# Two sums of each block of the second feed-forward weight, made in DRAM by GpSimd's DMAs

## Chip, cores and metric

The kernel runs on one core of a Trainium2 chip. The core has a matrix engine (TensorE, PE in the rows), VectorE (DVE), ScalarE (ACT), GpSimd (POOL), SyncE (SP) and 16 DMA engines that all queues share. The metric is the device time of one execution in microseconds (us). Every engine works through its own list of instructions in order; an instruction that waits holds all that stand behind it on that engine. A DMA that adds to its destination is issued from POOL.

## What is computed

One decoder layer on 512 tokens of width 2048, in float32:

```python
proj = jnp.einsum("bsd,de->bse", x, w_in[l])
q, k, v, gate_b, gate_c, h = jnp.split(proj, split_pts, axis=-1)
q, k = rope(q), rope(k)
attn = sliding_window_gqa(q, k, v, attn_sinks[l])
conv = gate_b * causal_depthwise_conv(gate_c * h, short_conv_w[l])
y = jnp.einsum("bsm,md->bsd", jnp.concatenate([attn, conv], -1), w_out[l])
x = layer_norm(DEEPNORM_ALPHA * x + y, ln1_g[l], ln1_b[l])
u = causal_depthwise_conv(jnp.einsum("bsd,df->bsf", x, ffn_w_up[l]), ffn_conv_w[l])
a, g = jnp.split(u, 2, axis=-1)
y = jnp.einsum("bsf,fd->bsd", jax.nn.silu(a) * g, ffn_w_down[l])
x = layer_norm(DEEPNORM_ALPHA * x + y, ln2_g[l], ln2_b[l])
```

## The kernel before

Every float32 operand is split into a high and a low part (`split`, L181 to L184: ScalarE casts `whi`, then VectorE subtracts to get `wlo`), and a product is three matmuls. Weights come as chunks of 1 MB, 128 x 2048, in the DRAM tensor `ws`. SP loads them into three `raw` buffers (`dma_to`); four pairs of `whi`/`wlo` hold 1024 columns each, so PE has at most four halves of a chunk prepared.

The stages are these. First the projection to q, in two panels of eight halves, with the one for k and v (four halves) between them. Each of the three ends with the rotation (`rope`, L249 to L261): per token block VectorE writes `wa` and `wb` from PSUM and POOL adds them into `qm` (for q) or `kr` (for k). `wa` and `wb` have two buffers each, so VectorE cannot begin the third token block before POOL has added the first. Then follow the convolution's projections, 48 halves, with attention woven in: attention's first step (`att_q`) splits `qm`, and PE transposes the parts `qs` right behind the first of the 48 halves. Then come the output projection, LayerNorm, the up-projection, and the down-projection with the second LayerNorm.

Up- and down-projection use seven products in place of eight on a 2 x 2 block of sub-matrices (Strassen's scheme in Winograd's form). In the down-projection a block `n` (10 of them, `NB`) has four weight chunks, w0 to w3, and products 1 to 7. Products 1, 2 and 3 use w0, w1 and w2. Product 5 uses w3 + w0, product 6 adds w2 to that, product 4 adds w1 to that, and product 7 uses w3 + w2. The products run in the order 1, 2, 6, 3, 7, 5 of the next block, 4.

Before the change the sums are made in SBUF. `d_load` has POOL load w3 into a buffer `wqd` and add w0 by two DMAs (`d_add`, half a chunk each). For product 6 VectorE adds w2 from its `raw` buffer (L566), once for each half. For product 4 POOL adds w1 by DMA. For product 7 SP loads w3 into a `raw` buffer and POOL adds w2 by two DMAs there.

The order of instructions on each engine is fixed when the program is built, by a scheduler that estimates when each could run; a DMA call stands in the program where that scheduler sets it, not where the Python line is.

Of the kernel before, what the change touches and what calls it, by code (L numbers as in the profile page):

```python
# [8 lines left out]
F32 = mybir.dt.float32  # L9
F32R = mybir.dt.float32r  # L10
AF = mybir.ActivationFunctionType
ALU = mybir.AluOpType
AX = mybir.AxisListType

P = 128
S = 512
D = 2048
# [21 lines left out]
C_DOWN = C_UP + 2 * NF  # L39
ND = NF // 4  # L40
NB = 2 * (NF // 8)
C_TAIL = C_DOWN + 4 * NB
# [75 lines left out]
class Kernel:  # L118
# [19 lines left out]
    def dma_to(self, c):  # L138
        nc = self.nc
        while self.next_dma <= min(c, NCHUNK - 1):  # L140
            i = self.next_dma
            t = self.p_raw.tile([P, 2048], F32, name="raw")
            self.raw[i] = t
            self.next_dma += 1

            cuts = {0: (512, 1024, 1536, 2048), 1: (1024, 2048)}.get(i, (2048,))
            c0 = 0
            for c1 in cuts:
                nc.sync.dma_start(t[:, c0:c1], self.ws_d[i][:, c0:c1])
                if i == 0:  # L150
                    k = c0 // 512 % 2
                    self.load_x(slice(k, k + 1), nc.scalar if c0 < 1024 else nc.sync)
                else:
                    self.load_x()
                c0 = c1
            if C_UP <= i < C_DOWN and (i - C_UP) % 2:
                self.w_add(t[:, 1024:], (i - C_UP) // 2, 1, 0)
            if C_DOWN <= i < C_TAIL and (i - C_DOWN) % 4 == 3:
                for h in range(2):
                    self.d_add(t, (i - C_DOWN) // 4, 2, h)  # L160

    def load_x(self, ks=slice(0, 2), queue=None):
        if self.x_at < KT // 2:
# [378 lines left out]
    def d_add(self, t, n, i, h):  # L542

        c = slice(1024 * h, 1024 * (h + 1))
        self.nc.gpsimd.dma_start(t[:, c], self.ws_d[C_DOWN + 4 * n + i][:, c], accum_op=ALU.add)

    def d_load(self, n):

        if n < NB:
            t = self.wq[n] = self.p_qd.tile([P, 2048], F32, name="wqd")  # L550
            self.nc.gpsimd.dma_start(t, self.ws_d[C_DOWN + 4 * n + 3])
            for h in range(2):
                self.d_add(t, n, 0, h)

    def down_prep(self, n, p, h):

        if p in (5, 6, 4):
            src = self.wq[n]
        else:
            c = C_DOWN + 4 * n + (1, 2, 3, 7).index(p)  # L560
            self.dma_to(c + 2)
            src = self.raw[c]
        hi, lo = self.hl_tiles()
        cs = slice(1024 * h, 1024 * (h + 1))
        if p == 6:
            self.nc.vector.tensor_tensor(src[:, cs], src[:, cs], self.raw[C_DOWN + 4 * n + 2][:, cs], op=ALU.add)  # L566
        self.split(hi, lo, src[:, cs])
        self.hl[n, p, h] = (hi, lo)
        if p == 6:
            self.d_add(src, n, 1, h)  # L570
        elif h and p == 4:
            del self.wq[n]
            self.d_load(n + 2)
        elif h and p in (1, 2, 3, 7):
            del self.raw[c]
# [147 lines left out]
    def run(self):  # L723
        nc, tc = self.nc, self.tc
# [17 lines left out]
        p_d = opened("spill", 1, space=bass.MemoryType.DRAM)  # L742
        self.hd = [p_d.tile([P, 4, S], F32, name=f"hd{u}") for u in range(ND)]
        zd = [p_d.tile([P, D], F32, name=f"zd{tb}") for tb in range(NTB)]
        self.x_at, self.xraw = 0, {}
        self.dma_to(2)

# [59 lines left out]
        for i in range(2 * NC_CONV):  # L807
            j = 2 * C_CONV + i
            q = i % 4
            if q == 0:  # L810
                pss = [self.psum("mm") for _ in range(2)]
            hi, lo = self.half(j, 4)
            self.feat_half(hi, lo, q, pss)
            if q == 3:
                self.conv_evac(i // 4, pss)
            for u, off in ((i, 0), (i - 1, 1), (i - 4, 2), (i - 5, 3)):
                if u % 2 == 0 and 0 <= u // 2 < 16:
                    n = u // 2
                    if off == 0:
                        st[n] = self.att_q(*units[n])  # L820
                    elif off == 1:
                        st[n] = self.att_scores(*units[n], st[n])
                    elif off == 2:
                        st[n] = self.att_transpose(*units[n], st[n])
                    else:
                        self.att_values(*units[n], st.pop(n))
# [10 lines left out]
        for k in (slice(0, 2), slice(2, 8)):  # L837
            for tb in range(NTB):
                sl = slice(tb * P, (tb + 1) * P)
                src = self.qm[tb].rearrange("p (k t) -> p k t", t=P)  # L840
# [75 lines left out]
        n = len(self.order)  # L916
# [28 lines left out]
        for i, (m, p, h) in enumerate(self.todo[n:]):  # L945
            self.prepare(n + i + 4)
            u, c = divmod(m, 2)
# [8 lines left out]
            if u + 1 < NB // 2:  # L956
                at, q = (1, {3: 4, 7: 5, 4: 1, 11: 2, 12: 6, 16: 3, 13: 7})
                if u == 0:
                    at, q = (3, {4: 4, 11: 5, 12: 1, 16: 2, 13: 6, 17: 3, 14: 7})
# [17 lines left out]
            k = end.index((m, p))  # L977
# [41 lines left out]
```

## Time and profile before

| | |
|---|---|
| median of 3 runs | 2019.3 us (2015.41 to 2021.93) |
| the profiled execution | 2018.78 us |
| its span, first to last instruction | 2016.7 us |
| mean granted TensorE clock | 0.980 |
| PE busy | 1928.5 us (96%) |
| DVE, ACT, POOL busy | 1405.6, 918.8, 286.3 us |
| DMA moved | 398.73 MB, 198 GB/s over the span |

A row of a timeline gives start, length, engine, line and operation, and in brackets the idle time before it and what ended that. A row of the windows gives for a stretch how long each engine was busy, the granted clock, the mean busy share of the 16 DMA engines and the rate they moved. The table of queues gives packets, megabytes and the share of the 16 engines' time: q0 holds the DMAs that POOL issues, q1 those of SP and ACT.

### The profile page before, as it was taken

How to read it: one execution, taken by the hardware profiler on the slowest of the kernel's cores; microseconds unless marked ns; L12 is line 12 of the kernel's file. 1: busy time of each engine (PE TensorE's matmuls, PEld its weight loads, DVE VectorE, ACT ScalarE, POOL GpSimd, SP SyncE). 2: the span in 40 equal slices, each digit the busy share in tenths (PEclk: the TensorE clock that was granted, in tenths of full speed). 3: DMA queues.
4: the chain of work that ended last, by engine and by line, in shares of the span. 5: the costliest groups of instructions: out<-in, count | busy, mean ns of one | idle time of the engine just before them, and what ended most of it. 6: DMA issues, size and time to landing. Idle time of an engine off the chain costs nothing. (4 is left out here: it accounts for less than half of the span.)

```text
span 2016.7 us, 25991 instructions
## 1 busy us (share of the span) xinstructions
PE 1928.5 (96%) x9950; PEld 1638.4 (81%) x9950; DVE 1405.6 (70%) x2001; ACT 918.8 (46%) x1403; POOL 286.3 (14%) x315
## 2 busy tenths in 40 slices
PE   9999999999994899999999999999997989999887
PEld 7988888888893788888888888888885778787766
DVE  5357676353358777777777777777777778787777
ACT  4234444232124555555555555555555544344331
POOL 1110000000033111111111111111111111111104
PEclk9999999999996999999999999999998999999989
DMA  6222122552234599999999999999998868888762
GB/s 264 101 88 84 63 84 75 156 219 94 105 110 130 145 263 253 266 240 263 250 258 259 243 261 248 262 246 258 255 238 238 247 194 242 220 233 245 237 188 84
DMA packets 93499, 398.73 MB, mean 198 GB/s; under 512 B 9472, under 2 KB 20768, under 8 KB 67520
## 3 DMA queue, kind: packets, MB, share of 16 engines
q0 software_dynamic: 36256, 139.11, 36.2%
q1 hardware_dynamic: 56544, 256.92, 34.2%
q8 instruction: 78, 1.28, 0.2%
q10 hardware_dynamic: 576, 1.05, 0.1%
q14 instruction: 45, 0.37, 0.0%
HBM read 377.12 MB, written 19.92 MB: 197 GB/s over the span
## 5 line engine op out<-in xcount | busy, mean ns | idle before, releaser
L184 DVE TENSOR_TENSOR wlo<-raw,whi 128x1024 fp32r<-128x1024 f32 (+1 forms) x358 | 438.2, 1227 | 293.2 <-ACT whi L183 292.8
L183 ACT CAST whi<-raw 128x1024 fp32r<-128x1024 f32 (+1 forms) x358 | 373.5, 1045 | 574.9 <-PE mm L216 118.3
L482 PE MATMUL mm<-act,whi 128*128 128x512 f32 x1072 | 385.0, 400 | 0.0
L484 PE MATMUL mm<-act,wlo 128*128 128x256 f32 x1072 | 302.1, 282 | 0.0
L482 PE MATMUL aux<-x,whi 128*128 128x512 f32 x704 | 252.7, 395 | 20.9 <-DVE x L184 20.0
L482 PEld LDWEIGHTS mm<-act,whi 128*128 128x128 f32 x1072 | 202.7, 189 | 49.7 <-DVE mt L490 0.2
L434 POOL DMA_DIRECT2D wq<-ws x132 | 129.5, 983 | 726.0 <-DVE wlo L184 605.7
L184 DVE TENSOR_TENSOR wlo<-wq,whi 128x1024 fp32r<-128x1024 f32 x132 | 161.1, 1223 | 98.6 <-ACT whi L183 98.4
L484 PEld LDWEIGHTS mm<-act,wlo 128*128 128x128 f32 x1072 | 204.0, 190 | 0.4 <-DVE wlo L184 0.3
L183 ACT CAST whi<-wq 128x1024 fp32r<-128x1024 f32 x132 | 138.2, 1050 | 139.4 <-PE mm L482 50.3
L484 PE MATMUL aux<-x,wlo 128*128 128x256 f32 x704 | 199.6, 284 | 0.0
L482 PEld LDWEIGHTS aux<-x,whi 128*128 128x128 f32 x704 | 133.1, 189 | 52.1 <-DVE x L184 20.3
L214 PE MATMUL mm<-act,whi 128*128 128x512 f32 x384 | 151.5, 394 | 0.0
L216 PE MATMUL mm<-act,wlo 128*128 128x512 f32 x384 | 150.1, 391 | 0.0
L215 PE MATMUL mm<-act,whi 128*128 128x512 f32 x384 | 149.6, 390 | 0.0
L484 PEld LDWEIGHTS aux<-x,wlo 128*128 128x128 f32 x704 | 133.2, 189 | 0.2
L482 PE MATMUL mm<-x,whi 128*128 128x512 f32 x352 | 125.5, 393 | 2.3 <-DVE m L490 1.2
L614 PE MATMUL mm<-whi,act 128*128 128x512 f32 x256 | 103.5, 405 | 21.4 <-DVE z L630 21.4
L482 PE MATMUL aux<-act,whi 128*128 128x512 f32 x336 | 120.4, 398 | 0.0
L214 PE MATMUL mm<-whi,act 128*128 128x512 f32 (+1 forms) x316 | 116.5, 369 | 0.0
L216 PE MATMUL mm<-whi,act 128*128 128x512 f32 (+1 forms) x316 | 116.2, 368 | 0.0
L215 PE MATMUL mm<-wlo,act 128*128 128x512 f32 (+1 forms) x316 | 116.2, 368 | 0.0
(202 smaller groups left out, 3837.0 us busy)
## 6 DMA issues: line engine op xcount, KB each, us to landing
raw<-ws SPq DMA_DIRECT2D x180, 1024.0 KB, 8.2
wq<-ws POOLq DMA_DIRECT2D x132, 512.0 KB, 9.3
raw<-ws POOLq DMA_DIRECT2D x64, 512.0 KB, 7.6
wq<-ws SPq DMA_DIRECT2D x44, 512.0 KB, 8.2
wqd<-ws POOLq DMA_DIRECT2D x40, 512.0 KB, 13.2
hd<-ca SPq DMA_DIRECT2D x44, 256.0 KB, 10.0
h<-hd SPq DMA_DIRECT2D x22, 512.0 KB, 12.8
wqd<-ws POOLq DMA_DIRECT2D x10, 1024.0 KB, 5.1
```

The lines of the kernel that those rows point to most:

```text
L183: self.nc.scalar.copy(hi, src)
L184: self.nc.vector.tensor_tensor(lo, src, hi.bitcast(F32), op=ALU.subtract)
L214: mm(ps, sh, mh, start=start, stop=False)
L215: mm(ps, sh, ml, start=False, stop=False)
L216: mm(ps, sl, mh, start=False, stop=stop)
L434: self.nc.gpsimd.dma_start(dst, self.ws_d[C_UP + 2 * f + i][:, 1024 * j:1024 * (j + 1)], accum_op=ALU.add)
L482: mm(ps, hi[:, sl], x[:, k, :, :].rearrange("p a t -> p (a t)"), start=new and k == 0, stop=False, skip_group_check=not new)
L484: mm(ps[:, :H], lo[:, sl], x[:, k, 0, :], start=False, stop=k == 7, skip_group_check=not new)
L614: mm(ps[b], xh, hi[:, k, :], start=new and h == 0 and k == 0, stop=False, **kw)
```

## The change

Twenty tensors `sum0_5`, `sum0_7`, ..., `sum9_7` of 1 MB each are set up in DRAM. `w_sum` copies w3 of a block from `ws` to such a tensor (one DMA) and adds w0 or w2 to it (two DMAs of half a chunk), all issued from POOL, DRAM to DRAM: 20 copies and 40 adds. It is called in the loop over the convolution's 48 halves. `d_load` then loads w3 + w0 in one DMA, and SP loads w3 + w2 in place of w3. VectorE's add of w2 for product 6 becomes two DMA adds on POOL, issued when product 5's halves are split.

```diff
             for c1 in cuts:
-                nc.sync.dma_start(t[:, c0:c1], self.ws_d[i][:, c0:c1])
+                n, q = divmod(i - C_DOWN, 4)
+                src = self.sums[n, 7] if C_DOWN <= i < C_TAIL and q == 3 else self.ws_d[i]
+                nc.sync.dma_start(t[:, c0:c1], src[:, c0:c1])
...
-            if C_DOWN <= i < C_TAIL and (i - C_DOWN) % 4 == 3:
-                for h in range(2):
-                    self.d_add(t, (i - C_DOWN) // 4, 2, h)
...
+    def w_sum(self, k):
+
+        s = k // 2 if k % 2 == 0 else (k - 3) // 2
+        if not 0 <= s < 2 * NB:
+            return
+        n, p = s // 2, (5, 7)[s % 2]
+        w = lambda i: self.ws_d[C_DOWN + 4 * n + i]
+        if k % 2 == 0:
+            self.nc.gpsimd.dma_start(self.sums[n, p], w(3))
+        else:
+            for h in range(2):
+                c = slice(1024 * h, 1024 * (h + 1))
+                self.nc.gpsimd.dma_start(self.sums[n, p][:, c], w(0 if p == 5 else 2)[:, c], accum_op=ALU.add)
+
     def d_load(self, n):
 
         if n < NB:
             t = self.wq[n] = self.p_qd.tile([P, 2048], F32, name="wqd")
-            self.nc.gpsimd.dma_start(t, self.ws_d[C_DOWN + 4 * n + 3])
-            for h in range(2):
-                self.d_add(t, n, 0, h)
+            self.nc.gpsimd.dma_start(t, self.sums[n, 5])
...
-        if p == 6:
-            self.nc.vector.tensor_tensor(src[:, cs], src[:, cs], self.raw[C_DOWN + 4 * n + 2][:, cs], op=ALU.add)
         self.split(hi, lo, src[:, cs])
         self.hl[n, p, h] = (hi, lo)
-        if p == 6:
+        if p == 5:
+            self.d_add(src, n, 2, h)
+        elif p == 6:
             self.d_add(src, n, 1, h)
...
+        self.sums = {(n, p): p_d.tile([P, D], F32, name=f"sum{n}_{p}") for n in range(NB) for p in (5, 7)}
...
             self.feat_half(hi, lo, q, pss)
+            self.w_sum(i - 2)
```

POOL's list before, from the last of the small loads at the start to the rotation of k (`qm` and `kr` are the sums of the rotation):

```order
L777 DMA fcw<-fcw 128x264
L261 TENSOR_TENSOR qm_169<-wa,wb 128x512
L261 TENSOR_TENSOR qm_170<-wa,wb 128x512
L261 TENSOR_TENSOR qm_171<-wa,wb 128x512
L261 TENSOR_TENSOR qm_172<-wa,wb 128x512
L261 TENSOR_TENSOR kr<-wa,wb 128x128 x4
```

POOL's list with the change, ending at the first two of the same additions (the load of `fcw` and the copies to `sum_5_106` and `sum_7_107` stand just ahead of these rows; L554 is a copy, L558 the adds):

```order
L558 DMA sum_5_106<-ws 128x1024 x2
L554 DMA sum_5_108<-ws 16x16384
L558 DMA sum_7_107<-ws 128x1024 x2
L554 DMA sum_7_109<-ws 16x16384
L558 DMA sum_5_108<-ws 128x1024 x2
L554 DMA sum_5_110<-ws 16x16384
L558 DMA sum_7_109<-ws 128x1024 x2
L554 DMA sum_7_111<-ws 16x16384
L558 DMA sum_5_110<-ws 128x1024 x2
L554 DMA sum_5_112<-ws 16x16384
L260 TENSOR_TENSOR qm_189<-wa,wb 128x512
L260 TENSOR_TENSOR qm_190<-wa,wb 128x512
```

Seven copies and the adds of five sums now stand ahead of the rotation of the first q panel. Each first half of an add waits for its copy to land.

POOL's list with the change further on, up to the rotation of the second q panel:

```order
L554 DMA sum_7_119<-ws 16x16384
L558 DMA sum_5_118<-ws 128x1024 x2
L554 DMA sum_5_120<-ws 16x16384
L558 DMA sum_7_119<-ws 128x1024 x2
L554 DMA sum_7_121<-ws 16x16384
L558 DMA sum_5_120<-ws 128x1024 x2
L554 DMA sum_5_122<-ws 16x16384
L558 DMA sum_7_121<-ws 128x1024
L260 TENSOR_TENSOR qm_189<-wa,wb 128x512
L260 TENSOR_TENSOR qm_190<-wa,wb 128x512
```

By here 17 of the 20 copies and the adds of 15 sums and a half are issued; `sum_7_121` is the 16th sum. All this stands ahead of the convolution's first half.

VectorE's list in the down-projection before, at product 6 of one block (`z` takes the products, L630):

```order
L630 TENSOR_TENSOR z_13503<-z_13503,mm 128x512
L630 TENSOR_TENSOR z_13504<-z_13504,mm 128x512
L566 TENSOR_TENSOR wqd<-wqd,raw 128x1024
L184 TENSOR_TENSOR wlo<-wqd,whi 128x1024
L566 TENSOR_TENSOR wqd<-wqd,raw 128x1024
L184 TENSOR_TENSOR wlo<-raw,whi 128x1024
L630 TENSOR_TENSOR z_13503<-z_13503,aux 128x512
L630 TENSOR_TENSOR z_13504<-z_13504,aux 128x512
```

The same place with the change:

```order
L641 TENSOR_TENSOR z_13583<-z_13583,mm 128x512
L641 TENSOR_TENSOR z_13584<-z_13584,mm 128x512
L183 TENSOR_TENSOR x_5099<-h_14209,x_5099 128x4x256
L183 TENSOR_TENSOR wlo<-wqd,whi 128x1024
L596 TENSOR_TENSOR h_14209<-h_14209,h_14213 128x1024
L183 TENSOR_TENSOR wlo<-raw,whi 128x1024
L641 TENSOR_TENSOR z_13583<-z_13583,aux 128x512
L641 TENSOR_TENSOR z_13584<-z_13584,aux 128x512
```

The two additions from `raw` are gone from VectorE, here and in the nine other blocks.

## Rows read from the trace of the kernel before

**Rows 1.** The page, busy time of PE: us, share, instructions.

```profile
PE   1928.5 (96%) x9950; PEld 1638.4 (81%) x9950; DVE 1405.6 (70%) x2001; ACT 918.8 (46%) x1403; POOL 286.3 (14%) x315
```

**Rows 2.** Windows: the first two projections' stretches, and the down-projection.

```profile
core 0: us, PE busy (x) PEld busy (x) DVE busy (x) ACT busy (x) POOL busy (x), PEclk, DMA share, GB/s
0.00:47.00 47.00, 45.06 (x189) 34.97 (x190) 23.62 (x31) 21.77 (x30) 4.57 (x15) 1.00 0.72 283
47.00:116.00 69.00, 69.00 (x403) 61.03 (x402) 24.55 (x50) 16.73 (x27) 8.85 (x8) 1.00 0.26 92
...
1560.00:1950.00 390.00, 365.50 (x1560) 296.17 (x1559) 304.35 (x321) 170.92 (x174) 51.40 (x62) 0.98 0.81 231
```

**Rows 3.** Waits, down-projection: engine, line, waited for, us, times, longest.

```profile
DVE wqd L566 <- DMA raw<-ws: 27.4, 5, 7.9
```

**Rows 4.** Timelines of DVE and PE at one of these waits.

```profile
1656.09 2.36 DVE L566 TENSOR_TENSOR wqd<-wqd,raw 128x1024 f32<-128x1024 f32 x2 [7.13 <-DMA raw<-ws]
...
1660.33 0.48 PE L614 MATMUL mm<-whi,x 128*128 128x512 f32 x1 [3.98 <-DVE z L630]
```

**Rows 5.** Windows around PE's four stalls behind that wait, and one earlier.

```profile
1504.00:1528.00 24.00, 14.60 (x78) 11.93 (x77) 14.68 (x19) 10.14 (x15) 4.69 (x6) 0.87 1.05 338
...
1652.00:1664.00 12.00, 8.03 (x31) 6.28 (x30) 7.91 (x9) 3.44 (x4) 0.57 (x1) 0.90 0.29 107
1732.00:1748.00 16.00, 11.20 (x41) 8.73 (x41) 9.73 (x11) 4.26 (x5) 0.56 (x1) 0.86 0.40 156
1820.00:1828.00 8.00, 4.31 (x20) 3.25 (x19) 4.26 (x5) 3.05 (x3) 0.00 (x0) 1.00 0.34 144
1864.00:1872.00 8.00, 4.65 (x21) 3.59 (x20) 3.53 (x5) 2.13 (x3) 0.00 (x0) 1.00 0.30 128
```

**Rows 6.** Timelines of POOL, ACT and PE where the down-projection begins.

```profile
1506.39 1.11 POOL L551 DMA_DIRECT2D wqd<-ws  x2 [5.29 <-PE mm L484]
1515.08 1.82 POOL L545 DMA_DIRECT2D wqd<-ws  x2 [7.58 <-DMA wqd<-ws]
...
1520.38 1.99 ACT L183 CAST act<-h 128x1024 fp32r<-128x1024 f32 x2 [0.50 <-DMA h<-hd]
...
1526.47 1.22 PE L614 MATMUL aux<-whi,act 128*128 128x512 f32 x2 [9.36 <-ACT whi L183]
```

**Rows 7.** Timeline of POOL, from the start to the up-projection's first add.

```profile
4.62 0.54 POOL L777 DMA_DIRECT2D fcw<-fcw  x1
49.64 2.55 POOL L261 TENSOR_TENSOR qm<-wa,wb 128x512 f32<-128x512 f32 x2 [44.48 <-DVE wb L259]
...
73.32 0.46 POOL L261 TENSOR_TENSOR kr<-wa,wb 128x128 f32<-128x128 f32 x1 [17.39 <-DVE wb L259]
...
117.40 2.56 POOL L261 TENSOR_TENSOR qm<-wa,wb 128x512 f32<-128x512 f32 x2 [38.54 <-DVE wb L259]
...
356.50 0.91 POOL L434 DMA_DIRECT2D wq<-ws  x1 [233.61 <-DVE wlo L184]
```

**Rows 8.** Timelines of DVE and PE at the second q panel's rotation.

```profile
118.74 0.69 DVE L256 TENSOR_TENSOR wa<-mm,rope_t 128x512 f32<-128x512 f32 x1 [0.15 <-POOL qm L261]
...
121.27 0.48 DVE L310 TENSOR_TENSOR qs<-qm,qs 128x256 fp32r<-128x256 f32 x1
...
123.64 0.46 PE L313 MATMUL aux<-identr,qs 128*128 128x128 f32 x4
```

**Rows 9.** DMA queues: 700 to 1500 us (two rows), then 366 to 392 us.

```profile
q0 software_dynamic: 23449, 85.38, 60.2%
q1 hardware_dynamic: 23328, 116.66, 39.0%
...
q0 software_dynamic: 288, 1.05, 24.1%
```

**Rows 10.** Issues, whole span: transfers, KB each, median us to landing.

```profile
wqd<-ws POOLq DMA_DIRECT2D x40, 512.0 KB, 13.2
...
wqd<-ws POOLq DMA_DIRECT2D x10, 1024.0 KB, 5.1
...
zd<-z SPq DMA_DIRECT2D x4, 1024.0 KB, 4.4
```

## The prediction

> **What bounds the kernel now.** I first read the busy times: PE works 96% of the span [rows 1], so time can be won only where PE stands still or at its lower clock, and any new stall of PE is lost in full. The windows then show where: from the start to 116 us PE loses only 2 us, all at its beginning, while the down-projection (1560 to 1950 us) leaves PE 390 - 365.5 = 24.5 us idle [rows 2]. The waits there name VectorE's add L566, which waits 27.4 us in five goes for w2's `raw` load [rows 3]. VectorE works in order, so behind that add stand the reads of PSUM (L630), and PE waits for these: L566 sits 7.1 us until 1656 and PE loses 4.0 us until 1660 [rows 4]. Four such stalls are in the windows: 12 - 8.0, 16 - 11.2, 8 - 4.3 and 8 - 4.7, together 15.8 us [rows 5]. One more stall of 9.4 us stands where the down-projection begins [rows 5, 6].
>
> Second, I read what the change needs: room on the DMA engines and in POOL's list. The DMA share is 0.72 up to 47 us, nearly all SP's first loads, and 0.26 up to 116 us [rows 2], and POOL works little. But POOL's additions for the rotation stand at 49.6, 73.3 and 117.4 us [rows 7], and VectorE's third `wa` ends its wait on the first of them at once: 0.15 us [rows 8]. There is no slack between POOL and VectorE here.
>
> **The change, part by part. What it saves.** L566 leaves VectorE, and so do its waits. Product 6 now takes its addend by DMA adds issued when product 5 is split, four products or about 24 us earlier (the stalls of [rows 5] at 1656, 1740 and 1824 us stand two blocks apart, so a block takes 42 us and a product 6); an add of half a chunk lands in 13.2 us [rows 10], so it is hidden; if it were late it would show as the same stall. w2 itself is next needed one product later, 6 us, against waits at L566 of 27.4 / 5 = 5.5 us, so what comes late next is small. I take the full 15.8 us. At the beginning of the stage POOL loaded w3 at 1506.4, could add w0 only at 1515.1, and PE began at 1526.5 [rows 6]. Now one load does. The next thing late is the activations `h`, whose casts run at 1520.4 to 1522.4 [rows 6]; the weight's split could be ready before that, so I count 6 of the 9.4 us. The clock: around these stalls the mean grant is 0.86 to 0.90 [rows 5], that is some us at the lower level of 1.2 GHz; three such dips, some 1 us each, give 3. **Saved: 15.8 + 6 + 3 = 25 us**, from 14 (if a later w2 or `h` takes half of the first two terms back) to 36 (if the rest of the stage's idle time shrinks too, since 10 MB of adds less pass through the DMA engines).
>
> **What it adds.** Forty half adds and 20 copies, DRAM to DRAM. By its call the change puts them beside the convolution's 48 halves. The list of POOL says otherwise: nothing in them waits for a half, and the scheduler has placed them from the load of `fcw` on, ahead of the rotations. POOL is free at 4.6 + 0.5 = 5.2 us [rows 7]. It starts the copies then, in the middle of SP's first loads, and it cannot do the second q panel's rotation until the adds of the 16th sum are issued, which wait for the 16th copy. In order of issue 16 copies and the adds of 14 sums lie ahead of that point.
>
> Each transfer's price, in time of all 16 engines. SP's plain loads, beside the adds of the up-projection: 116.66 MB in 39.0% of 800 us, so a chunk of 1.05 MB takes 2.8 us. POOL's adds into SBUF: 85.38 MB in 60.2%, so a chunk takes 5.9 us, and alone, from 366 to 392 us, 24.1% of 26 us = 6.3 [rows 9]. No row shows a copy or an add with both ends in DRAM. A copy costs between 2.8 (a load; a store to DRAM of the same size lands in 4.4 us, a load in 5.1 [rows 10]) and 5.6 (a load's and a store's legs one after the other); I take the middle, 4.2. An add of a chunk costs between 2.8 (as a load, if its second read were free) and 5.9 + 2.8 = 8.7 (one more leg through DRAM); I take 5.9, the same operation with another destination.
>
> So POOL's transfers ahead of the second rotation take 16 x 4.2 + 14 x 5.9 = 150 us of all engines. The engines also serve the other loads up to there, 0.72 x 47 + 0.26 x 69 = 52 us [rows 2]. Together with the start at 5.2 us and 2 us for the last copy to be reported landed (5.1 - 2.8, [rows 9, 10]), POOL comes to the rotation at 5 + 150 + 52 + 2 = 209 us, in place of 117.4 [rows 7]: 91 us later. The work adds up whichever queue is served first, since between them both always have something to move: an add is issued while the adds before it still run, and POOL's issue of one takes 0.9 us [rows 7].
>
> Who waits: VectorE's third `wa` waits for POOL's addition; behind it on VectorE stand the split for `qs` and all later `wlo`. PE has the first convolution half prepared, does it, and stops at the transposes of `qs`, which come in the next place of its list, at 123.6 us [rows 8]. `qs` is ready at 121.3 + 0.5 = 121.8 now, so PE has 1.8 us of slack. **PE is late by 91 - 2 = 89 us** when it passes there. It doesn't matter for the sum how this divides over earlier places: the first rotation is passed at 5 + 5 x 4.2 + 3 x 5.9 + SP's share, some 75 us in place of 49.6, which the four prepared halves of the k and v panel partly hide; the rotation of k, behind nine copies and seven sums, some 130 in place of 73.3. What is stalled there isn't stalled again at the end. The clock adds to it: two or three long stalls, each followed by some us at 1.2 GHz as in [rows 5], about 4 us. After that point five adds and three copies are left, 42 us of DMA beside loads that take a quarter of the engines' time; POOL's next duty is at 356 us [rows 7] and PE's loads come well ahead, so this rest is free.
>
> The Trainium skill's page "DMA: Bandwidth & Descriptors" (section "Latency and other measured facts") gives 207 to 214 GB/s per direction for copies between HBM tensors at full rate. By that a copy would take an estimated 5.0 us, and the sum above would be 13 us longer; no run here shows it.
>
> **Sum.** 89 + 4 - 25 = +68 us, on the profiled execution's 2018.8 us: **2087 us**. That execution lies 0.5 us under the median of the runs, so nothing is to be corrected.
>
> **The rivals.**
>
> First, the sums are cheap and the kernel ends level or faster. One mechanism: an add in DRAM at the price of a plain load. Then 16 x 2.8 + 14 x 2.8 = 84, POOL arrives at 143 us, 26 late, PE 24 late, against 25 saved: 2018 us. Faster begins where POOL is at the second rotation before some 143 us, that is where copy and add of a chunk take together less than 5.6 us. For it: DMA engines that work on two queues could hide one's latency behind the other. Against it: the adds in SBUF took 5.9 us both beside other traffic and alone 6.3 [rows 9]. If they overlapped wholly with SP's loads, 52 us would fall out of the first sum, and with 2.8 us for each, POOL is in time and the whole 25 us are won: 1994.
>
> Second, the sums are dear. 16 x 5.6 + 14 x 8.7 = 211, POOL arrives at 270, 153 late: 2018.8 + 151 + 4 - 25 = 2149. For it: both reads and the write of an add go to DRAM. Against it: stores and loads land about equally soon [rows 10].
>
> Third, the change does what its call says: the sums run beside the convolution and hold up nothing. Then only the saving is left, 2018.8 - 25 = 1994 us. POOL's list in the built program speaks against it: the additions of the rotation stand behind the sums in a list that is worked in order.
>
> Fourth, copies of 64 KB to a row crowd SP's loads out at the start, and PE starves for x before any rotation. It changes the place of the stall, not the sum, unless SP's loads come last; then PE's work up to the second rotation (117 us) begins late, and it ends as in the second rival.
>
> **How the numbers follow.** The forecast (PE late by 45 to 120 us) has a chance of 0.70; it spans 2043 to 2118, with a copy of 2.8 and adds of 5.9 at 16 x 2.8 + 14 x 5.9 = 127 us: 2064. The dear case with the fourth rival: 0.15. The cheap case: 0.10, of which 0.04 within 0.3% (6 us, about what a measurement of this kernel can tell from no change), 0.03 faster and 0.03 still slower. The third rival and full overlap: 0.05. So slower 0.88, same 0.04, faster 0.08. The range reaches from 2036, part of the way to the cheap case, to 2140, most of the way to the dear one.
>
> **What would show it.** In the profile after: POOL's `qm` additions of the second panel near 209 us and not 117; L558 waiting for L554's copies in POOL's waits; VectorE waiting for POOL at `wa` (L255); PE idle between 60 and 210 us in two or three stretches with a lower clock behind them; DMA share near 1 from 5 to 210 us; no stalls of PE at distances of 84 us in the down-projection, and its length some 25 us shorter. Wrong would be: the rotations in their old places, or a DMA table in which q0's copies and adds take a time for each MB far from 4.2 and 5.9 us.

## The result, and the profile after

The changed kernel takes 2049.4 us (median of 4 runs, 2048.44 to 2051.39), the kernel before 2017.4 us beside it (4 runs, 2014.97 to 2021.93): a ratio of 1.0152, interval 1.0134 to 1.017. It is slower by 32 us. The forecast was 68 us slower, 2087 us; the time lies inside the range, nearer to its low end.

The page's first row, and the windows that answer to [rows 2]; one more stretch follows the first two, and the down-projection, which begins some 65 us later now, is cut in two where its early idle time ends:

```profile
PE   1931.9 (94%) x9950; PEld 1642.5 (80%) x9950; DVE 1390.2 (68%) x1981; ACT 920.7 (45%) x1403; POOL 310.5 (15%) x355
```

```profile
core 0: us, PE busy (x) PEld busy (x) DVE busy (x) ACT busy (x) POOL busy (x), PEclk, DMA share, GB/s
0.00:47.00 47.00, 37.12 (x129) 26.49 (x130) 14.12 (x20) 13.50 (x20) 14.15 (x29) 0.89 0.97 308
47.00:116.00 69.00, 58.15 (x325) 50.39 (x324) 25.73 (x48) 16.69 (x27) 18.94 (x24) 0.93 1.00 289
116.00:192.00 76.00, 39.40 (x183) 32.37 (x182) 20.28 (x28) 11.94 (x17) 21.42 (x27) 0.78 1.02 274
1560.00:1628.00 68.00, 56.94 (x266) 47.04 (x265) 52.84 (x65) 40.18 (x54) 5.49 (x7) 0.90 0.81 234
1628.00:1980.00 352.00, 352.00 (x1546) 290.07 (x1544) 285.50 (x300) 170.02 (x170) 36.87 (x46) 1.00 0.82 232
```

Two things are to be seen. Up to 192 us the DMA engines are full and PE stands still for 57 us (9.9 + 10.9 + 36.6), where it lost 2 us in 116 us before. Its matmuls ran at a mean grant of 0.78 to 0.93 there: the same 626 matmuls up to the transposes of `qs` were busy for 132.9 us in place of 121.7, which is another 11 us of its lateness (66.6 us, below). And in the down-projection PE works for 352 us without a gap, at the full clock of 2.4 GHz, where 390 us held 24.5 us of idle time. The DMA share there is what it was, 0.82 beside 0.81.

POOL's timeline after, against [rows 7]:

```profile
5.14 1.03 POOL L554 DMA_DIRECT2D sum<-ws  x2
...
31.36 1.66 POOL L558 DMA_DIRECT2D sum<-ws  x2 [12.45 <-DMA sum<-ws]
...
80.44 3.54 POOL L260 TENSOR_TENSOR qm<-wa,wb 128x512 f32<-128x512 f32 x2 [18.65 <-DVE wb L258]
...
111.72 0.73 POOL L260 TENSOR_TENSOR kr<-wa,wb 128x128 f32<-128x128 f32 x1
...
183.34 2.77 POOL L260 TENSOR_TENSOR qm<-wa,wb 128x512 f32<-128x512 f32 x2
```

The copies begin at 5.1 us, the adds (L558) wait for them, and the second panel's rotation comes at 183.3 us in place of 117.4. At 80.4 POOL waited for VectorE and not the other way round: there PE itself was late. The waits up to 260 us (engine, line, waited for: total us, times, longest):

```profile
POOL sum L558 <- DMA sum<-ws: 140.3, 18, 12.5
...
ACT act L182 <- DMA xraw<-xt: 39.2, 9, 9.7
...
PE aux L312 <- DVE qs L309: 36.6, 1, 36.6
...
DVE wa L255 <- POOL qm L260: 34.8, 1, 34.8
```

The last three are the two ways in which PE starved. First SP's loads of weights and of `x` come late, as the issues up to 100 us show (KB each, median us to landing). Before, eleven weight loads and the loads of `x`:

```profile
raw<-ws SPq DMA_DIRECT2D x11, 1024.0 KB, 5.0
xraw<-xt SPq DMA_DIRECT2D x6, 512.0 KB, 9.6
```

With the change eight weight loads, 26.8 us where the first eight of before took 6.7, and the loads of `x`:

```profile
raw<-ws SPq DMA_DIRECT2D x8, 1024.0 KB, 26.8
...
xraw<-xt SPq DMA_DIRECT2D x6, 512.0 KB, 31.9
```

PE was some 31 us late at the end of the first q panel for that (POOL's first addition at 80.4 us against 49.6). Then one wait of 36.6 us follows at the transposes of `qs`, behind POOL's list. They run at 190.2 us, 66.6 later than in [rows 8]. From there the lateness stays: the up-projection begins 69.0 us late (694.3 against 625.3). The down-projection begins 64.5 late (1591.0 against 1526.5) and its last product ends 30.0 late (1990.7 against 1960.7); the span is 31.2 us longer. So 69.0 us were lost and 37.8 won, 34.5 of these inside the down-projection. Its windows from the first matmul to the last, of before and then of after:

```profile
1526.47:1960.70 434.23, 402.24 (x1693) 325.43 (x1694) 342.05 (x363) 194.72 (x204) 54.92 (x66) 0.96 0.79 227
```

```profile
1591.04:1990.70 399.66, 391.66 (x1694) 321.52 (x1695) 325.38 (x345) 197.24 (x204) 40.37 (x50) 0.98 0.79 222
```

Idle time fell from 32.0 to 8.0 us, and the same matmuls were busy for 10.6 us less, at a mean grant of 0.98 in place of 0.96: fewer of them ran at 1.2 GHz behind a stall.

### The profile page after: what moved, and what is told of

It reads as the page before. It is cut to its first block, busy times and chain, and to the rows that moved or that the text cites. A ratio compares the mean times of both kernels' runs of the same rounds, so it can differ in the third digit from the quotient of the medians.

```text
span 2047.9 us, 26002 instructions
## 1 busy us (share of the span) xinstructions
PE 1931.9 (94%) x9950; PEld 1642.5 (80%) x9950; DVE 1390.2 (68%) x1981; ACT 920.7 (45%) x1403; POOL 310.5 (15%) x355
## 5 line engine op out<-in xcount | busy, mean ns | idle before, releaser
L213 PE MATMUL mm<-whi,act 128*128 128x512 f32 (+1 forms) x316 | 120.8, 382 | 17.8 <-ACT act L182 15.4
L215 PE MATMUL mm<-whi,act 128*128 128x512 f32 (+1 forms) x316 | 119.8, 379 | 0.0
L626 PE MATMUL mm<-wlo,act 128*128 128x512 f32 x256 | 101.0, 394 | 4.0 <-DVE wlo L183 4.0
```

The costliest lines, as they stand in the source:

```text
L213: mm(ps, sh, mh, start=start, stop=False)
L215: mm(ps, sl, mh, start=False, stop=stop)
L626: mm(ps[b], xh, lo[:, k, :], start=False, stop=False, **kw)
```

## The experiments: what was lost

The theory, as forecast (Q in the expectations): POOL's list holds the copies and adds ahead of the rotation, and their DMA time sets when PE goes on. The rival (D): the DMA traffic itself is dear wherever it runs.

**The sums behind the last addition of the rotation in POOL's list (e1_behind).** Nothing else differs.

```diff
-        nc.gpsimd.tensor_tensor(dst, t1, t2, op=ALU.add)
+        self.rot = nc.gpsimd.tensor_tensor(dst, t1, t2, op=ALU.add)
...
-            self.w_sum(i - 2)
+            with tc.issue_after(self.rot.ins):
+                self.w_sum(i - 2)
```

> The change as it is, but POOL's sums are queued behind the additions of the second q panel's rotation; nothing else differs. Theory Q (the sums cost time because they stand ahead of the rotations in POOL's list and beside SP's first loads): the whole loss at the start, 69 us at PE's first transposes of qs, goes, and the saving of 38 us stays: 2017 - 38 = 1979 us, transposes at 124 us as before the change. Rival D (20 copies and 40 adds in DRAM keep the DMA engines full for some 220 us wherever they stand, and PE starves for the convolution's loads): 2000 us or more, with PE idle between 125 and 380 us.

Measured: 1981.06 us, ratio to before 0.9817 (0.98 to 0.9834). It is faster than both kernels. The window over the stretch of the sums, which ran from 123 to some 332 us:

```profile
116.00:341.00 225.00, 225.00 (x1141) 189.42 (x1140) 158.04 (x327) 105.30 (x266) 48.63 (x64) 1.00 0.94 262
```

PE never stops while the DMA engines are 94% busy, so the traffic alone costs nothing there. Where the sums stand in POOL's list, and with it when they run, cost the 68 us.

**No sums in DRAM (e2_nosums).** The down-projection of the changed kernel with w3 in place of both sums.

```diff
-                src = self.sums[n, 7] if C_DOWN <= i < C_TAIL and q == 3 else self.ws_d[i]
+                src = self.ws_d[i]
...
-            self.nc.gpsimd.dma_start(t, self.sums[n, 5])
+            self.nc.gpsimd.dma_start(t, self.ws_d[C_DOWN + 4 * n + 3])
...
-            self.w_sum(i - 2)
```

> The change without the sums: no copy and no add in DRAM, product 5 and product 7 take w3 alone (w0 and w2 are left out of these two sums). It shows what the new down-projection saves by itself. By the two traces the stage from its first to its last main matmul takes 399.7 in place of 434.2 us, the transition saves 3.7 more and the tail loses 1.2: 2017 - 38 = 1979 us. By the forecast's own term of 25 us it would be 1992.

Measured: 1978.55 us, ratio 0.9808 (0.9788 to 0.9828). That is the saving alone, 39 to 40 us against the kernel before in its two sets of runs (2017.4 and 2018.5 us); the forecast's own term would have made it 1992.

**The sums alone (e3_sumsonly).** The kernel before, with the sums made and not used; `w_sum` and the tensors are those of the change.

```diff
...
+            self.w_sum(i - 2)
```

> The kernel before with the sums' copies and adds added and nothing read from them: the loss alone. Theory Q: PE passes the first transposes of qs 69 us late and nothing is given back: 2017 + 69 = 2086 us. If part of the 38 us came from somewhere else than the new down-projection (from work that now lies better after the long stall), it would be less, say 2070.

Measured: 2086.19 us, ratio 1.0338 (1.0311 to 1.0365). Its waits:

```profile
PE aux L313 <- DVE qs L310: 36.3, 1, 36.3
```

```profile
PE mm L628 <- DVE z L644: 25.3, 9, 6.1
```

The first is the lost time at the transposes as in the changed kernel, the second the old stalls of the down-projection, unchanged. Loss (+68) and saving (-39) are separate and add up within some 4 us.

**The rotation's additions on VectorE (e4_rotdve).** POOL's list then holds nobody up.

```diff
-        nc.gpsimd.tensor_tensor(dst, t1, t2, op=ALU.add)
+        nc.vector.tensor_tensor(dst, t1, t2, op=ALU.add)
```

> The change with the rotation's additions moved from POOL to VectorE, so that nobody waits for POOL's list; the sums still start at 5 us beside SP's first loads. Theory Q: the wait of 36 us at the transposes of qs goes and the delay of the first q panel (PE finishes it at 78 in place of 47 us, for want of x) stays, 31 us: 2017 + 31 - 38 = 2010 us. If POOL's list alone were the cause: 1979. If the crowded loads alone were the cause: 2049 still.

Measured: 2013.15 us, ratio 0.9976 (0.9959 to 0.9994). The wait for POOL is gone and the transposes run at 155.9. What is left is the crowding of SP's first loads (wait of PE up to 260 us, and the window up to 80 us, where PE was busy for 78.06 us in the kernel before):

```profile
PE mm L213 <- ACT act L182: 16.1, 4, 5.4
```

```profile
0.00:80.00 80.00, 59.24 (x194) 43.20 (x195) 23.93 (x31) 21.61 (x30) 18.66 (x35) 0.85 1.00 312
```

**The sums behind the first panel's rotation (e7_first).** The opposite: SP's first loads are left alone, and the second rotation still stands behind sums. `self.rot` is set as in e1_behind.

```diff
...
         self.q_evac(q0, 0)
+        rot0 = self.rot
...
-            self.w_sum(i - 2)
+            with tc.issue_after(rot0.ins):
+                self.w_sum(i - 2)
```

> The sums queued behind the rotation of the first q panel, so SP's first loads run undisturbed; ahead of the second rotation stand eleven copies and the adds of nine sums. Theory Q: POOL begins at 54 us, nine copies and seven adds (70 us at the price measured) and the loads' quarter bring it to the second rotation at about 144 us in place of 117: PE 25 us late there: 2017 + 25 - 38 = 2004 us. If only the crowded first loads mattered: 1980. If the lists were no matter and only the work counted: 1980 too, so 2004 speaks for the list alone.

Measured: 2008.96 us, ratio 0.9961 (0.9943 to 0.9978). POOL's four additions of the second panel (first and last start at the row's end), and PE's wait:

```profile
L260 POOL TENSOR_TENSOR qm<-wa,wb x4: 1717/1779/1835, 145.6 to 155.0; 128x512 f32<-128x512 f32 x4
```

```profile
PE aux L312 <- DVE qs L309: 26.5, 1, 26.5
```

So the two causes are each enough for some 30 us, and one number orders all of these kernels, the start of the transposes of `qs`:

| kernel | transposes, us | later than e1_behind | time, us | more than e1_behind |
|---|---|---|---|---|
| e1_behind | 123.7 | | 1981.1 | |
| e7_first | 150.4 | 26.7 | 2009.0 | 27.9 |
| e4_rotdve | 155.9 | 32.2 | 2013.2 | 32.1 |
| the changed kernel | 190.2 | 66.5 | 2049.4 | 68.4 |

What PE loses before that point arrives at the end within 2 us.

**The price of a copy (e5_copies).** As e1_behind, the copies alone.

```diff
-            for h in range(2):
-                c = slice(1024 * h, 1024 * (h + 1))
-                self.nc.gpsimd.dma_start(self.sums[n, p][:, c], w(0 if p == 5 else 2)[:, c], accum_op=ALU.add)
+            pass
```

> As e1_behind, with the 20 copies only; the 40 adds in DRAM are left out, so products 5 and 7 use w3 alone. It measures a copy by itself beside the convolution's loads, whose share of the DMA engines is 0.26. In e1_behind a sum took 8.2 us of all engines (q0 79.6% of 205 us, 20 sums). By the forecast's split (4.2 and 5.9) 20 copies would take 84 us of q0's time, by the load's price of 2.8 us 56, by 5.6 us 112. PE is not touched: 1978 to 1982 us.

Measured: 1981.59 us in one run. The queue of POOL from 123 to 205 us, in which the 20 copies ran (packets, MB, share of 16 engines), and SP's loads beside them:

```profile
q0 software_dynamic: 640, 20.97, 71.8%
```

```profile
raw<-ws SPq DMA_DIRECT2D x7, 1024.0 KB, 24.1
```

20 copies took 0.718 x 82 = 58.9 us of all engines, 2.9 us for each.

**The price of an add (e6_twice).** As e1_behind, each add issued twice.

```diff
+                self.nc.gpsimd.dma_start(self.sums[n, p][:, c], w(0 if p == 5 else 2)[:, c], accum_op=ALU.add)
```

> As e1_behind, with each of the 40 adds in DRAM made twice (the sums hold w0 or w2 twice). The time of q0 that is added over e1_behind is the price of 20 adds of a chunk: 118 us if an add costs 5.9 us as in SBUF, 56 if it costs as little as a load. The sums then end some 280 to 350 us after their start, at up to 480 us, still ahead of the up-projection at 625 us: 1978 to 1985 us.

Measured: 1983.99 us in one run. POOL's queue over the whole span, e1_behind and then e6_twice:

```profile
q0 software_dynamic: 39776, 170.57, 43.1%
```

```profile
q0 software_dynamic: 45536, 191.54, 48.9%
```

0.489 x 1982.2 - 0.431 x 1979.5 = 116 us for 20 chunks more: 5.8 us for an add of a chunk with both ends in DRAM. In e1_behind itself all sums took 79.6% of 125 to 330 us, 163 us; less the copies that is 5.2 us for each.

## The experiments: what was won

The forecast put the saving on L566 and took 25 us; it was 38. Three theories were tried: L566 itself delays PE (S); the adds, as traffic on the DMA engines, make the loads late (T); the adds that POOL issues into SP's `raw` buffers for product 7 do it (U).

**The kernel before, with product 6's add by DMA alone (e8_add6).**

```diff
-        if p == 6:
-            self.nc.vector.tensor_tensor(src[:, cs], src[:, cs], self.raw[C_DOWN + 4 * n + 2][:, cs], op=ALU.add)
...
-        if p == 6:
+        if p == 5:
+            self.d_add(src, n, 2, h)
+        elif p == 6:
```

> The kernel before with one part of the change alone: w2 is added for product 6 by POOL's DMAs when product 5 is split, not by VectorE; the sums for products 5 and 7 are made in SBUF as before, so the down-projection moves 10 MB more through adds, not 10 MB less. If the stalls behind L566 are the saving (15.8 us of idle time and the clock behind them): 1995 to 2000 us. If what saves is the traffic taken away (adds for product 7 into the raw buffers, landing in 10.9 us, and those at the transition), nothing or a loss: 2015 us or more, as the DMA engines would be 0.93 busy in place of 0.79.

Measured: 2007.82 us, ratio 0.9951 (0.9932 to 0.997), between the two expectations. PE's wait in the down-projection:

```profile
PE mm L614 <- DVE z L630: 19.2, 4, 9.8
```

L566 is gone and four waits are left: three of 3.0 to 3.2 us and one of 9.8 at the stage's end. In the profiled execution (2004.7 us, the shortest of the seven) the stage takes 420.5 us from its first to its last product in place of 434.2, with 24.5 us of idle time in place of 32.0, at a DMA share of 0.94 in place of 0.79. So putting DMA adds in L566's place brings, by itself, some 10 us of the 38.

**Both sums from DRAM, VectorE's add kept (e9_keep566).**

```diff
+        if p == 6:
+            self.nc.vector.tensor_tensor(src[:, cs], src[:, cs], self.raw[C_DOWN + 4 * n + 2][:, cs], op=ALU.add)
...
-        if p == 5:
-            self.d_add(src, n, 2, h)
-        elif p == 6:
+        if p == 6:
```

> As e1_behind, but VectorE adds w2 for product 6 again (L566 of before), and the two DMA adds per block that took its place are left out: both sums still come ready from DRAM. It divides the down-projection's saving, some 38 us in e1_behind against before. Theory S (as the forecast counted it: L566 itself is the trouble, 15.8 us of stalls and 3 to 10 us of clock): its waits return in full, about 1981 + 16 + 8 = 2005 us, and VectorE's wait at L566 is again over 20 us. Rival T (the trouble is the adds on the DMA engines, which make w2 late; ready sums take them away): L566 finds w2 there, its waits are under 5 us, and the time is 1977 to 1983 us.

Measured: 1978.63 us, ratio 0.9809 (0.9786 to 0.9832). VectorE's add (now L577) and the window:

```profile
DVE wqd L577 <- DMA raw<-ws: 2.5, 2, 2.3
```

```profile
1560.00:1940.00 380.00, 377.44 (x1655) 310.30 (x1654) 324.40 (x346) 175.43 (x177) 26.28 (x32) 1.00 0.60 191
```

The instruction stays, its waits go, and PE loses nothing by it. L566 alone was not the trouble; S falls as it stood, since the gain comes without taking L566 away.

**Product 7's sum from DRAM, product 5's made in SBUF, no L566 (e10_only7).**

```diff
+        if p == 5:
+            return
...
-            self.nc.gpsimd.dma_start(t, self.sums[n, 5])
+            self.nc.gpsimd.dma_start(t, self.ws_d[C_DOWN + 4 * n + 3])
+            for h in range(2):
+                self.d_add(t, n, 0, h)
```

> As e1_behind, but only product 7's sum comes from DRAM; product 5's is made in SBUF as in the kernel before (one load, two DMA adds by POOL per block), so ten chunk adds of 5.9 us are back in the down-projection, and at its beginning POOL again loads w3 and then adds w0. Theory S (L566's removal is the gain, the adds on the DMA engines cost nothing): only the transition's some 4 to 6 us are lost, 1985 to 1987 us. Rival T (the adds make loads late and so PE idle): half of the relief is lost, waits of PE for VectorE's reads of PSUM return in part, and the time is 1992 to 2005 us.

Measured: 1982.56 us, ratio 0.9835 (0.9809 to 0.9862).

```profile
1560.00:1940.00 380.00, 377.42 (x1650) 310.53 (x1649) 304.53 (x325) 175.44 (x177) 51.97 (x63) 1.00 0.84 238
```

The DMA share is higher than before the change (0.84 against 0.81), and PE still loses only 2.6 us in these 380: T falls too as it stood, three adds per block and a share of 0.84 do not stall PE by themselves.

**Product 7's sum alone, all else as before (e11_sum7).** As e10_only7, with VectorE's add and without the DMA adds that replaced it, as in the diff of e9_keep566.

> The kernel before with product 7's sum alone read ready from DRAM (the ten sums behind the last addition of the rotation); product 5's sum is made in SBUF and VectorE adds w2 for product 6, both as in the kernel before. Theory U, from the two runs before: what delays PE in the down-projection are the adds that POOL issues into SP's raw buffers for product 7, which wait for the load and hold a raw buffer for longer; then this part alone brings nearly the whole saving: 1979 to 1986 us, and VectorE's wait at L566 is under 5 us. Theory S (L566) or T (traffic of the adds) would leave L566's waits or most of the traffic: 1998 to 2010 us.

Measured: 1982.26 us, ratio 0.982 (0.98 to 0.9839). VectorE's add:

```profile
DVE wqd L581 <- DMA raw<-ws: 4.7, 4, 1.7
```

**All but product 7's sum (e12_not7).**

```diff
-                src = self.sums[n, 7] if C_DOWN <= i < C_TAIL and q == 3 else self.ws_d[i]
+                src = self.ws_d[i]
...
+            if C_DOWN <= i < C_TAIL and (i - C_DOWN) % 4 == 3:
+                for h in range(2):
+                    self.d_add(t, (i - C_DOWN) // 4, 2, h)
...
+        if p == 7:
+            return
```

> The counterpart: as e1_behind, but product 7's sum is made as in the kernel before (SP loads w3 into a raw buffer, POOL adds w2 there by two DMAs), while product 5's sum comes ready from DRAM and L566 is gone. By theory U nearly the whole saving goes: 1995 to 2010 us, with PE waiting for VectorE's reads of PSUM again, some 15 us or more. By theory S or T it stays: 1980 to 1988 us, since L566 is gone and ten chunk adds fewer pass through the DMA engines than in the kernel before plus L566's.

Measured: 1987.12 us, ratio 0.9848 (0.9831 to 0.9864). POOL's wait for the load into the `raw` buffer is there again, as long as in the kernel before (71.1 us in four goes), and PE hardly minds:

```profile
POOL raw L547 <- DMA raw<-ws: 68.0, 6, 15.2
...
PE mm L630 <- ACT act L185: 6.0, 1, 6.0
```

U falls as well as it stood: product 7's sum is enough (e11_sum7), but most of the saving comes without it, where U foretold 1995 us or more. Together the runs read as follows (adds of a chunk per block in the down-projection; how many of them go into SP's `raw` buffers; PE's idle time from the stage's first to its last product):

| kernel | DMA adds per block | of these into `raw` | VectorE's add | PE idle, us | time, us |
|---|---|---|---|---|---|
| e9_keep566 | 1 | 0 | yes | 8.0 | 1978.6 |
| e11_sum7 | 2 | 0 | yes | 6.5 | 1982.3 |
| e1_behind | 2 | 0 | no | 8.0 | 1981.1 |
| e10_only7 | 3 | 0 | no | 6.7 | 1982.6 |
| e12_not7 | 3 | 1 | no | 11.4 | 1987.1 |
| before | 3 | 1 | yes | 32.0 | 2017 to 2020 |
| e8_add6 | 4 | 1 | no | 24.5 | 2007.8 |

Where product 7's sum comes ready, neither VectorE's add nor a third DMA add matters, and taking away both (e1_behind) brings no more than either. PE loses much in two kernels only: in the kernel before, with three adds, one of them into `raw`, and a VectorE that waits for w2 in the middle of its list, and in e8_add6, with four adds, one of them into `raw`, and no such VectorE.

Whether the number of adds decides, or that one of them goes into `raw`, stays open: all three kernels above 8.0 us of idle time have that one, and no run keeps it and VectorE's add while product 5's adds go. The landings fit the order of the table: SP's loads of 1 MB from `ws` landed at the median in 13.4 us (e8_add6) and 10.4 (before) between 1560 and 1900 us, and in 6.6 to 8.8 in the five others. Whether they are late as the cause or as a consequence of the stalls is not shown.

## Why the prediction was right in its sign and too high in its size

The way in which the change loses time was forecast rightly. The steps that failed are two terms of the sum: the price of a copy, taken as 4.2 us and measured at 2.9, and the saving, put on L566 at 25 us and measured at 38; DMA adds in L566's place bring some 10 by themselves (e8_add6).

**What bounds the kernel, and POOL's list: right.** Slower, forecast with a chance of 0.88, is what came. Each microsecond that PE lost ahead of the transposes came out at the end. The place of the sums in POOL's list made the loss: the same traffic from 123 us on costs nothing (e1_behind), while beside SP's first loads it is enough for 32 us by itself (e4_rotdve). The signs that the forecast named are there: L558 waiting for the copies, the third `wa` for POOL, a DMA share of 1.00 and 1.02, PE idle in stretches with a clock of 0.78 to 0.93 behind them.

**The copy: mis-sized.** The forecast had 2.8 us (a load) and 5.6 us as bounds and took the middle, 4.2; it is 2.9. The nearest row, the load, was the right one. For 16 copies that is 21 us too much, the larger part of the miss on this side. The page "DMA: Bandwidth & Descriptors" of the Trainium skill (section "Latency and other measured facts") gives 207 to 214 GB/s per direction for copies of tiles between HBM tensors at two of its row pitches, issued from other queues than POOL's. By that a copy would take an estimated 5.0 us; the 2.9 us measured here, in another layout, don't agree with it, and by it the sum would have been worse.

**The add: right within an eighth.** 5.9 forecast, 5.2 to 5.8 measured. The sum ahead of the second rotation can be read directly, from the queues between 5 and 183 us in the changed kernel:

```profile
q0 software_dynamic: 4931, 32.64, 71.8%
q1 hardware_dynamic: 3648, 18.94, 29.1%
```

POOL's 32.64 MB are 31 chunks, where 30 were counted. They took 0.718 x 178 = 128 us where 150 were forecast, SP's 0.291 x 178 = 52, as forecast. Their sum and the start at 5 us give 185; POOL came at 183.3 and not at 209. PE was 66.6 us late at the transposes, not 89.

**The clock after the stalls: right in size.** Between the transposes and the up-projection 2.4 us were added, all of it as busy time of PE (493.5 us against 491.2); 4 were forecast. **Lost, all told: 69.0 us where the forecast had 93.**

**The saving: mis-sized, and its cause told too simply.** 25 us were forecast and 38 won. The transition gave 3.7 and not 6 (PE's wait of 9.4 us in [rows 6] became 5.7). The idle time within the stage fell by 24.0 us, where 15.8 were counted for four stalls. The forecast followed L566 alone, while PE's waits on VectorE's reads in the stage, and one wait of ScalarE at its end, already showed more in the kernel before:

```profile
PE mm L614 <- DVE z L630: 25.4, 8, 7.3
```

```profile
1945.78 1.04 ACT L183 CAST act<-raw 128x1024 fp32r<-128x1024 f32 x1 [7.78 <-DMA raw<-ws]
```

The longest of the eight, 7.3 us, ends at 1953 us. It is not behind L566 but behind this cast, which waits for a late `raw` load; VectorE waits 5.8 us for the cast, and its reads of PSUM stand behind that. With the change 2.6 us of the stall are left. The clock gave 10.6 us where 3 were counted for the three windows that showed a dip. The upper end that the forecast gave, 36, was near. And L566 could have stayed: with product 7's sum ready its waits go while it remains (4.7 us left in e11_sum7, 2.5 in e9_keep566, of 27.4).

**The sum.** 66.6 + 2.4 - 37.8 = 31.2 us on the span. Against 68, that is 24 us less lost and 13 us more won. Both errors go the same way.

**The rivals.** The first (sums as cheap as loads) fell on the add, though it held for the copy. The second (dear sums) fell. The third, that the change does what its call says, was refused by POOL's list; e1_behind is the kernel that it describes, and it gave 1981, not 1994. The fourth, crowding of SP's first loads, took place: about 31 of the 67 us at the transposes are lost there. As the forecast said it moved the stall and does not seem to have lengthened the sum. POOL itself stood for 18.7 us up to 80.4 us, waiting for VectorE, but the DMA engines were full throughout (71.8% and 29.1% above), and POOL came to the second rotation where the sum of DMA time puts it. No run with this list and undisturbed first loads tests that. The crowding decides where POOL's list is free, as in e4_rotdve.

## What to carry to other kernels

A DMA that waits for nothing goes to wherever the scheduler finds its queue free, so look at what compute stands behind it in that engine's list, and add up the DMA time of everything ahead of it; setting it behind the last urgent instruction turned a loss of 32 us into a gain of 37. When a stall is to be removed, count all idle time of the waiting engine in that stage and the clock that it costs, not only the stalls of the line that you found. A line that waits may become harmless when something else is changed, so try the parts of a change apart: product 7's sum alone was worth as much as the whole down-projection's edit.

## What the runs showed of the hardware that was not expected

- A copy of 1 MB from DRAM to DRAM took 2.9 us of all 16 engines, what a load into SBUF took (2.8 in [rows 9]). An add in DRAM took 5.2 to 5.8 us, much as an add into SBUF (5.9 and 6.3).
- How late a load on SP's queue lands does not follow from the share of POOL's queue alone. A 1 MB load landed in 24.1 us beside copies alone (POOL's queue at 71.8%), in 12.2 us in e1_behind (79.6%, copies and adds, from 125 to 330 us), and in 26.8 us beside copies and adds at the start; from 125 to 330 us in the kernel before it is 4.7. In e5_copies POOL issued eight copies at once, in e1_behind two, and each copy's rows in the list are 64 KB long (16x16384). Whether the number under way or the length is the reason was not tried. The Trainium skill says in "DMA: Bandwidth & Descriptors" (section "Issuing engines are not separate DMA queues") that DMAs of all issuing engines run on the same 16 engines and interleave. The landings here agree.
- A DMA share of 0.94 (e1_behind, 116 to 341 us) left PE without a single gap; the same 0.94 in the down-projection of e8_add6 left it 24.5 us idle in 420. The share alone doesn't tell whether a load will be late.
